# Taking the level products of a gated linear recurrence in two halves of 64 stationary columns

## The chip, the cores and the metric

The kernel runs on one core of one Trainium2 chip. The metric is the device time of one execution in microseconds (us). Engines: TensorE (PE in the profile; its weight loads are a row of their own, PEld), VectorE (DVE), ScalarE (ACT), GpSimd (POOL), and SyncE (SP), which issues most DMAs.

## The reference: what is computed

A decoder trunk of two layers on x of 512 tokens by 1024 channels, float32. Layer 0 mixes tokens by an mLSTM and channels by a dense SwiGLU; layer 1 mixes tokens by an HGRN2 recurrence and channels by eight SwiGLU experts of which each token takes two. The part that matters here is the recurrence of layer 1, eight heads with keys and values of 128. In the reference, cut to what matters:

```python
def hgrn2_chunkwise(q, k, log_f, v):
    def step(s_st, xs):
        qc, kc, gc, vc = xs
        bc = jnp.cumsum(gc, axis=2)
        diff = bc[:, :, :, None, :] - bc[:, :, None, :, :]
        decay = jnp.exp(jnp.where(mask[:, :, None], diff, NEG))
        a = jnp.einsum('bhtd,bhsd,bhtsd->bhts', qc, kc, decay)
        o = (jnp.einsum('bhtd,bhdv->bhtv', qc * jnp.exp(bc), s_st)
             + jnp.einsum('bhts,bhsv->bhtv', a, vc))
        ...
```

The scores a[t, s] need a decay per channel d between tokens s and t, so they aren't one matrix product.

## The kernel before, in words

**Whole program.** Activations lie channel by token, 512 tokens in the free dimension. Each float32 weight block is split into two float32r parts (whi on ScalarE, wlo on VectorE), and a product of weights and activations is three matmuls with 512 columns. `Weights` (line 165) loads the blocks through SyncE's queue in the order of use and emits their splits. [...]

**The HGRN stage** (`hgrn`, line 1014, some 680 to 930 us of the span). `proj` (line 1071) is the main stream of wide matmuls: projections in the order v0, h2, h4, v1, h6, g0, g4 (names hv, hh, hg in the trace), then the output product h_out. After each pair of heads is projected, `evac` (line 1040) makes q, k, and the log of the forget gate summed within chunks of 128 tokens. `core` (line 1124) is one head's recurrence: it is emitted in steps between those of the main stream.

**A head's levels.** Within a chunk, the scores are built by halves: for n = 1, 2, 4, ..., 64, the pairs whose s lies in the left half and t in the right half of a block of 2n tokens. The seven levels are run by `skew` in four stages. `l0` (line 1160): E, two VectorE subtractions of 128x256 and an exp on ScalarE. `l1_` (line 1173): M = E times the left halves' k and the right halves' q, one VectorE instruction of 128x512. `l2_` (line 1179): for each of the four chunks one float32 product into the PSUM tile lp (al in the trace). Its stationary operand is the chunk's 128 columns of M (for n = 1, of k), its moving operand the 64 columns of right halves, and its result 128 x 64. For n = 64 only the 64 left columns are stationary. `l3` (line 1193): a copy of the wanted entries of lp into A by a mask, VectorE, 128x256. A float32 matmul shows as two records in the trace, each with a load of its own.

After the levels come the outputs (o) and the state (su, St) chunk by chunk, a norm by head on ScalarE, a transposition (tph), and hh, the head's operand of h_out. `heads` (line 1250) splits hh into hhi (ScalarE) and hlo (VectorE).

**What sets the order.** `weave` (line 336) emits the main stream and, between its steps of six wide matmuls, steps of up to three heads. It goes by `Plan` (line 270), which adds up the cost of what it gave to each engine:

```python
        if engine == "tensor":
            return n * (1.667 if out.dtype == F32 and ins[0].dtype == F32 else 0.417) * 1e-3
```

where n is the number of columns of the matmul's output. VectorE is charged 0.07 us and 1.04 or 0.53 ns per column, by the operands. A head's step is emitted if its previous step ends by the plan 0.3 us before TensorE's clock, and if the plan's VectorE and ScalarE are less than 3 us behind TensorE's:

```python
            late = max(t["vector"], t["scalar"]) - t["tensor"]
            if not x[2] and x[0] <= t["tensor"] + slack and late < backlog:
```

**Another place with halves.** In the mLSTM's `pair` (line 837), line 897 writes two products of 64 stationary columns to `cu[0:64]` and `cu[64:128]`.

All instructions of TensorE, VectorE and ScalarE go through one helper (line 317), so the trace tells them apart by tile and not by line.

Of the kernel before, what the change touches and what calls it, by code (L numbers as in the profile page):

```python
# [19 lines left out]
DRAM = bass.MemoryType.DRAM  # L20
# [17 lines left out]
# ---------------------------------------------------------------- weight order  # L38
# Every product's weights are cut into [128, 128] blocks and laid out in the order of use.
# [46 lines left out]
# ---------------------------------------------------------------- column vectors  # L86
# [14 lines left out]
def _consts():  # L101
    """Constants that depend on shapes alone, side by side in columns."""
# [39 lines left out]
def moe_steps():  # L142
    """The experts' products in order: an expert's first gate and up tiles go before the last one's down."""
    for e in range(NE + 1):
        if e < NE:
            yield from (("g", e, f) for f in range(EARLY))
        if e:
            yield from (("d", e - 1, d) for d in range(KT))
        if e < NE:
            yield from (("g", e, f) for f in range(EARLY, ET))  # L150


def moe_order():
    """Loads of the experts' weights: slots of gate and up tiles, then of the down product."""
    for e in range(NE + 1):
        if e < NE:
            yield from ((e * MB // 8 + 2 * f, 2) for f in range(EARLY))
        if e:
            base = (e - 1) * MB // 8 + 2 * ET
            yield from ((base + i, min(2, ET - i)) for i in range(0, ET, 2))  # L160
        if e < NE:
            yield from ((e * MB // 8 + 2 * f, 2) for f in range(EARLY, ET))


class Weights:
    """The weight blocks, loaded in pairs of slots and split into two float32r parts each.

    A slot of eight blocks is also a tick: what `at` puts off is emitted with the split of a later slot."""
# [20 lines left out]
    def want(self, slot):  # L189
        """Splits up to this slot, as far as room is free; returns what is left to emit."""  # L190
# [19 lines left out]
    def at(self, n, f):  # L210
        """Emits f n ticks from now."""
        self.tasks.setdefault(self.now + n, []).append(f)
# [11 lines left out]
    def rush(self, n=8):  # L224
        """The next n splits as far as there is room, where much other work is to come. Nothing that uses a
        block is left to emit."""
# [7 lines left out]
    def get(self, b, n=1, last=True):  # L234
        """Blocks b to b + n in two parts. Their slot's room is free again after its last block's last use."""
# [22 lines left out]
def skew(n, *stages, back=False):  # L258
    """Stage s of item k goes with stage 0 of item k + s, after it or (back) before it."""
# [10 lines left out]
class Plan:  # L270
    """Estimates of when each engine would get done with what it was given; `weave` goes by them."""
# [35 lines left out]
class Engine:  # L307
    """An engine whose instructions the plan takes note of."""
# [15 lines left out]
class Core:  # L324
    """nc with its compute engines seen by a plan."""
# [10 lines left out]
def weave(plan, main, sides, lanes, slack, backlog):  # L336
    """Emits main and, between its steps, those of the sides, `lanes` of them at a time.

    A side is a pair: whether it can start, and its steps. A step goes when by the plan the one before is
    done about when the tensor engine gets to it, and the other engines aren't too far behind.  # L340
    A side that yields "wait" needs more of main first, and main that does needs more of the sides."""
# [46 lines left out]
class Kernel:  # L388
# [15 lines left out]
    # ------------------------------------------------------------ small helpers  # L404
# [18 lines left out]
    def rsqrt(self, v, pool, name):  # L423
        """v ** -0.5 of a small tile: the exponent's halving for a start, then Newton's steps."""
# [9 lines left out]
    def table(self, name):  # L434
        """Loads a table set of the scalar engine's functions; Exp and Ln go by the one they find."""
# [6 lines left out]
    def dump(self, name, tiles):  # L442
        """For tests: [P, n] tiles side by side into a DRAM output."""
# [19 lines left out]
    def mm2(self, acc, w, x, start, stop):  # L463
        """acc[:, 0] + acc[:, 1] is the product; x has its two parts side by side."""
# [4 lines left out]
    # ------------------------------------------------------------ start  # L469
# [23 lines left out]
    # ------------------------------------------------------------ conditioning  # L493
    def scale_of(self, l, i, s=slice(0, 8)):
        """A = (1 + scale) * norm_w, for a layer's i-th norm."""
# [3 lines left out]
    def times_c(self, out, t):  # L499
        """A column of the sums of t * silu(c) by row."""  # L500
# [5 lines left out]
    def ada_first(self, pool):  # L506
        """Stages for shift and scale of the first norm, a d-tile at a time."""
# [5 lines left out]
        # (1 + scale) * norm_w with the bias' share first  # L513
# [55 lines left out]
    # ------------------------------------------------------------ norm  # L569
    def square(self, k):  # L570
        """The squares that the next norm takes: those before the last d-tile's as a sum, and the last's."""
# [12 lines left out]
    def token_scale(self):  # L584
        """1 / sqrt(mean square + eps), a column by token tile."""
# [11 lines left out]
    def norm(self, l, i, before=()):  # L597
        """hn = x * rs * A + B by d-tile, split into two float32r parts."""
# [36 lines left out]
    # ------------------------------------------------------------ products  # L635
    def group_first(self, name, n, normed):
        """n accumulators in step with a norm's d-tiles."""
# [10 lines left out]
    def tile_ws(self, b, xs, acc):  # L648
        """One 128-column tile of a product, d-major: weights stationary."""
# [6 lines left out]
    def tile_tok(self, b, i, acc):  # L656
        """Token tile i by 512 columns: tokens stationary."""
# [11 lines left out]
    def out_proj(self, name, hh, l, side=lambda: None):  # L669
        """x += gate1 * (hh @ w_out); hh gives the operands in turn, or None where they aren't there yet.  # L670
        Steps of side go along at last."""
# [36 lines left out]
    def to_dmajor(self, tp, w, pool, name):  # L708
        """A head's d-major outputs, times w, split."""
# [7 lines left out]
    # ------------------------------------------------------------ layer 0: mLSTM  # L717
    def mlstm(self):
# [3 lines left out]
        with ExitStack() as ctx:  # L722
# [24 lines left out]
            # q, k: convolution over four taps, silu  # L747
# [12 lines left out]
            # gates: rows 0-7 input gates, 32-39 forget gates  # L760
# [76 lines left out]
            def pair(p):  # L837
                """Two heads; then their outputs, gated and d-major."""
# [94 lines left out]
            def close(h):  # L933
                """A head's outputs, normed and gated, d-major."""
# [32 lines left out]
    # ------------------------------------------------------------ layer 0: dense SwiGLU  # L967
# [45 lines left out]
    # ------------------------------------------------------------ layer 1: HGRN2  # L1013
    def hgrn(self):
# [3 lines left out]
        with ExitStack() as ctx:  # L1018
# [8 lines left out]
            # lower bound: softmax over the one layer, its running sum less the first  # L1027
# [12 lines left out]
            def evac(n, qf):  # L1040
                """Two heads' q, k, log f summed within chunks, and q * f of the odd tokens."""
# [11 lines left out]
                for s in range(2):  # L1053
# [5 lines left out]
                    # log f; the table's range is narrower than the floor's  # L1059
# [50 lines left out]
            def gated(hs):  # L1110
                """The gates of some heads, and the outputs that were there before them."""
# [7 lines left out]
            def sel(qk, h):  # L1119
                """By level h: k of the left halves and q of the right ones."""  # L1120
# [3 lines left out]
            def core(h):  # L1124
# [7 lines left out]
                # across chunks  # L1132
# [8 lines left out]
                # within chunks: the diagonal, then halves of 1, 2, 4, ... tokens  # L1141
# [37 lines left out]
                def l2_(i):  # L1179
# [8 lines left out]
                    m = 64 if n == 64 else P  # L1188
                    for c in range(NC):
                        nc.tensor.matmul(lp[:m, c * 64:(c + 1) * 64], left[:, c * P:c * P + m],  # L1190
                                         right[:, c * bn:(c + 1) * bn], start=True, stop=True)
# [15 lines left out]
                # outputs and state  # L1207
# [68 lines left out]
    # ------------------------------------------------------------ layer 1: experts  # L1276
    def router(self):
        """hn @ router = rs * (x @ (A * router)) + B @ router"""
# [7 lines left out]
    def pre_route(self, pool, lps, xt):  # L1286
        """The router's share of x @ router by token, and x by token, as x's d-tiles get done."""
# [6 lines left out]
        def logits(k):  # L1294
            """By expert: x's d-tiles before the last; by token: their sum turned, and the last."""
# [53 lines left out]
    def route(self, pool, lps, xt):  # L1349
        """Top two experts of a token, its gates, and its rows in the experts' lists."""  # L1350
# [31 lines left out]
        # the first expert's rows straight from x by token: a product picks them and scales them  # L1382
# [6 lines left out]
        def picks(e, i, w):  # L1389
            """Row by row, which of a tile's tokens is in it, times w."""  # L1390
# [7 lines left out]
        def spread():  # L1398
            """Tokens to their rows of the experts' lists."""
# [36 lines left out]
        def rest(sl, ok, gate):  # L1436
            # what goes past an expert's rows
# [16 lines left out]
            # gates and rows of the last expert's results, and of the others'  # L1454
# [56 lines left out]
    def overflow(self, xt):  # L1511
        """Tokens past their expert's rows: each expert on all tokens, with the gates of those alone."""
# [47 lines left out]
    def experts(self, xp, hp, wk, xt, pick, rest):  # L1560
# [6 lines left out]
        def fetch(e):  # L1567
            """An expert's rows."""
# [10 lines left out]
        def turn(e, k0, kn):  # L1579
            """Its rows d-major, scaled and shifted, in two parts."""  # L1580
# [32 lines left out]
        def act(e, f, gu):  # L1613
            """silu(gate) * up, in two parts."""
# [24 lines left out]
        def down(e, d, yp):  # L1639
            """gate2 times a d-tile of the result, its rows by token at last."""  # L1640
# [46 lines left out]
        def select():  # L1687
            """The last expert's rows as the columns of products that add them to their tokens."""
# [13 lines left out]
        def add(i, j):  # L1702
            """What the experts before the last give a token."""
# [45 lines left out]
    def finish(self, rp, xt, g, r):  # L1749
        """The last expert's share, and the final norm."""  # L1750
# [55 lines left out]
# ---------------------------------------------------------------- host: layout only  # L1806
# [54 lines left out]
```

## Time and profile before

| | |
|---|---|
| time, median of 3 runs | 1597.63 us (1595.0, 1597.63, 1610.0) |
| span of the profiled execution | 1596.0 us |
| time of the profiled execution around its span | not given by the page |
| mean granted clock of TensorE | 0.975 |
| TensorE busy | 1526.0 us, 96% |
| VectorE busy | 1087.0 us, 68% |
| ScalarE busy | 843.7 us, 53% |

A row of the timeline has the start in us from the span's start, the time from the start of its first instruction to the end of its last, the engine, the line, the operation, the tiles written and read, the rows and columns of the array in use, the moving operand or the load, and how many neighbouring instructions the row merges (x8). Ends of matmuls are modelled; starts are measured, so intervals are best taken from start to start.

### The profile page before, as it was taken

Reading aid. Unit: us, or ns where it says so; the run is one execution under the profiler, and the core shown is the slowest. Engines: PE = TensorE matmul, PEld = TensorE weight load, DVE = VectorE, ACT = ScalarE, POOL = GpSimd, SP = SyncE. Lnnn points to the kernel's source line nnn. Section 1 sums busy time; section 2 is a strip of 40 time slices with the busy share of each in tenths; the row PEclk is TensorE's granted clock in tenths of the full one; section 3 lists DMA queues with packets and bytes.
Section 4 is the critical chain, followed back from the end, with each engine's and each line's share of the span. In section 5 each row is a group of like instructions: output and inputs, shape, how many; then the busy total and the mean of one; then the engine's idle time right before and its main releaser. Section 6 shows DMA issues by size and latency. Waiting matters only on the chain. (4 is left out here: it accounts for less than half of the span.)

```text
span 1596.0 us, 23645 instructions
## 1 busy us (share of the span) xinstructions
PE 1526.0 (96%) x8991; PEld 1326.5 (83%) x8991; DVE 1087.0 (68%) x1981; ACT 843.7 (53%) x1560; POOL 118.5 (7%) x187
## 2 busy tenths in 40 slices
PE   4989989999999999999999998999999999999995
PEld 3866767788888888688888876999999999999994
DVE  6875684555445555595977644787877777787794
ACT  5463533432213322365656534777776767777663
POOL 0000000000000000300000010401001010100152
PEclk9999999999999999999999998999999999999996
DMA  9322452254455553532102132877777786877772
GB/s 378 149 96 90 145 191 100 105 219 178 171 195 182 191 194 111 206 141 89 54 28 79 54 133 88 332 258 276 266 261 275 251 294 227 292 257 251 275 284 89
DMA packets 79542, 297.30 MB, mean 186 GB/s; under 512 B 7732, under 2 KB 7780, under 8 KB 78400
## 3 DMA queue, kind: packets, MB, share of 16 engines
q1 hardware_dynamic: 69424, 266.36, 46.6%
q0 software_dynamic: 10000, 29.38, 5.3%
q8 instruction: 73, 1.20, 0.3%
q14 instruction: 45, 0.37, 0.1%
HBM read 277.64 MB, written 18.06 MB: 185 GB/s over the span
## 5 line engine op out<-in xcount | busy, mean ns | idle before, releaser
L317 DVE TENSOR_TENSOR wlo<-raw,whi 128x1024 fp32r<-128x1024 f32 x403 | 490.2, 1223 | 129.4 <-ACT whi L317 128.0
L317 ACT ACTIVATE whi<-raw 128x1024 fp32r<-128x1024 f32 x403 | 422.1, 1055 | 183.8 <-DMA raw<-in_w 39.4
L317 PE MATMUL gu<-x,whi 128*128 128x304 f32 x1408 | 359.0, 344 | 1.0 <-DVE x L317 1.0
L317 PE MATMUL gu<-x,wlo 128*128 128x152 f32 x1408 | 327.8, 233 | 0.0
L317 PEld LDWEIGHTS gu<-x,wlo 128*128 128x128 f32 x1408 | 269.0, 191 | 0.0
L317 PEld LDWEIGHTS gu<-x,whi 128*128 128x128 f32 x1408 | 264.3, 188 | 1.9 <-DVE x L317 1.1
L317 PE MATMUL yd<-h,whi 128*128 128x304 f32 x704 | 184.3, 350 | 2.8 <-DVE h L317 2.8
L317 PE MATMUL yd<-h,wlo 128*128 128x152 f32 x704 | 164.9, 234 | 0.0
L317 PEld LDWEIGHTS yd<-h,whi 128*128 128x128 f32 x704 | 133.9, 190 | 3.3 <-DVE h L317 3.2
L317 PEld LDWEIGHTS yd<-h,wlo 128*128 128x128 f32 x704 | 136.2, 194 | 0.0
L317 DVE SCALAR_TENSOR_TENSOR ar<-ar,cond 128x1024 f32<-128x1024 f32 x80 | 97.2, 1218 | 6.9 <-DMA ar<-in_ada 6.9
L317 ACT ACTIVATE fhi<-fg 128x512 fp32r<-128x512 f32 x22 | 13.9, 633 | 114.3 <-DVE fg L317 114.3
L317 DVE TENSOR_TENSOR fg<-fg,fup 128x512 f32<-128x512 f32 x20 | 13.8, 688 | 82.6 <-PE fup L317 82.6
L317 PE MATMUL fd<-fhi,whi 128*128 128x512 f32 x176 | 69.6, 396 | 0.0
L317 PE MATMUL fd<-flo,whi 128*128 128x512 f32 x176 | 69.6, 396 | 0.0
L317 PE MATMUL fd<-fhi,wlo 128*128 128x512 f32 x176 | 69.6, 396 | 0.0
L317 ACT ACTIVATE t<-gu 128x152 f32<-128x152 f32 x176 | 48.5, 288 | 34.5 <-PE gu L317 34.5
L317 PE MATMUL fgp<-lo,whi 128*128 128x512 f32 x160 | 62.3, 389 | 0.0
L317 PE MATMUL fgp<-hi,whi 128*128 128x512 f32 x160 | 62.2, 389 | 0.0
L317 PE MATMUL fgp<-hi,wlo 128*128 128x512 f32 x160 | 62.2, 389 | 0.0
L317 PE MATMUL fup<-hi,whi 128*128 128x512 f32 x160 | 62.2, 389 | 0.0
L317 PE MATMUL fup<-lo,whi 128*128 128x512 f32 x160 | 62.2, 389 | 0.0
(408 smaller groups left out, 3015.3 us busy)
## 6 DMA issues: line engine op xcount, KB each, us to landing
raw<-in_moe SPq DMA_DIRECT2D x128, 1024.0 KB, 5.3
raw<-in_w SPq DMA_DIRECT2D x69, 1024.0 KB, 4.9
ar<-in_ada SPq DMA_DIRECT2D x80, 512.0 KB, 4.2
ad<-in_ada SPq DMA_DIRECT2D x8, 1024.0 KB, 17.4
XG<-zero POOLq DMA_DIRECT2D x18, 256.0 KB, 5.9
raw<-in_moe SPq DMA_DIRECT2D x8, 512.0 KB, 3.5
xr<-XG POOLq DMA_DIRECT2D x14, 256.0 KB, 6.2
Y<-yt POOLq DMA_DIRECT2D x14, 256.0 KB, 3.8
```

What stands on the lines that cost most here:

```text
L317: r = f(*args, **kw)
```

## The change

The product of each chunk is issued for 64 columns of the stationary operand at a time: the first half writes partitions 0 to 63 of lp, the second 64 to 127. The moving operand is the same for both. For n = 64 the product stays one of 64 columns. The copies that read lp stay as they were. The rest of the diff takes out comments and docstrings.

```diff
                     lp = Ls[i] = self.ps(f"al{n}{h}", (P, 256))
                     bn = P // (2 * n)
-                    m = 64 if n == 64 else P
                     for c in range(NC):
-                        nc.tensor.matmul(lp[:m, c * 64:(c + 1) * 64], left[:, c * P:c * P + m],
-                                         right[:, c * bn:(c + 1) * bn], start=True, stop=True)
+                        for m in range(0, 64 if n == 64 else P, 64):
+                            nc.tensor.matmul(lp[m:m + 64, c * 64:(c + 1) * 64], left[:, c * P + m:c * P + m + 64],
+                                             right[:, c * bn:(c + 1) * bn], start=True, stop=True)
```

## Rows read from the trace of the kernel before

**Rows 1.** The page, busy time, share and instructions of the engines.
```profile
PE 1526.0 (96%) x8991; PEld 1326.5 (83%) x8991; DVE 1087.0 (68%) x1981; ACT 843.7 (53%) x1560; POOL 118.5 (7%) x187
```

**Rows 2.** Stretches: PE, PEld, DVE, ACT, POOL busy, granted clock, DMA share, GB/s.
```profile
700.00:720.00 20.00, 20.00 (x125) 17.37 (x124) 18.89 (x40) 10.16 (x15) 0.00 (x0) 1.00 0.15 54
720.00:740.00 20.00, 20.00 (x120) 17.30 (x119) 7.10 (x26) 5.72 (x26) 0.00 (x0) 1.00 0.15 54
...
920.00:940.00 20.00, 17.73 (x71) 13.90 (x71) 11.28 (x21) 9.36 (x23) 4.17 (x9) 0.91 0.51 177
```

**Rows 3.** Tile al: records, ns min/median/max, first and last start, forms.
```profile
L317 PE MATMUL al<-M x384: 217/275/325, 697.6 to 906.4; 128*128 128x64 f32 x160, 128*64 128x64 f32 x32
L317 PEld LDWEIGHTS al<-q,QK x64: 188/192/192, 695.2 to 876.5; 128*128 128x128 f32 x64
```

**Rows 4.** Timeline, ends of a stretch of 128 columns; ends and loads of one of 64.
```profile
715.07 0.39 PE L317 MATMUL hh<-hi,wlo 128*128 128x512 f32 x1
...
716.43 0.39 PE L317 MATMUL hh<-lo,whi 128*128 128x512 f32 x1
...
717.36 0.40 PE L317 MATMUL hh<-hi,wlo 128*128 128x512 f32 x1
717.68 0.54 PEld L317 LDWEIGHTS al<-M 128*64 128x64 f32 x8 [0.36 <-issue]
...
718.63 0.40 PE L317 MATMUL hh<-lo,whi 128*128 128x512 f32 x1
```

**Rows 5.** Timeline, a stretch of two 128-column groups.
```profile
707.34 0.40 PE L317 MATMUL hv<-whi,lo 128*128 128x512 f32 x1
...
707.58 1.89 PE L317 MATMUL al<-M 128*128 128x64 f32 x16
...
709.59 0.39 PE L317 MATMUL hv<-wlo,hi 128*128 128x512 f32 x1
```

**Rows 6.** Timeline of TensorE, the wide matmuls around the mixed stretch.
```profile
825.59 0.40 PE L317 MATMUL hh<-hi,wlo 128*128 128x512 f32 x1
...
827.75 0.40 PE L317 MATMUL hh<-lo,whi 128*128 128x512 f32 x1
```

**Rows 7.** Tile cu, loads (ns); then its first four records in three windows.
```profile
L317 PEld LDWEIGHTS cu<-va,kt x48: 132/134/137, 117.6 to 173.1; 128*64 128x64 f32 x48
...
117.63 0.20 PEld L317 LDWEIGHTS cu<-va,kt 128*64 128x64 f32 x4 [0.36 <-issue]
...
117.64 0.33 PE L317 MATMUL cu<-va,kt 128*64 128x129 f32 x2
...
117.69 0.14 PEld L317 LDWEIGHTS cu<-va,kt 128*64 128x64 f32 x2
```

**Rows 8.** Timeline of VectorE, the parts of a level's step and two M tiles.
```profile
714.77 0.43 DVE L317 COPY_PREDICATED A<-lvm,al 128x256 f32<-128x256 uint32 x1
...
715.10 0.68 DVE L317 TENSOR_TENSOR M<-E,QK 128x512 f32<-128x512 f32 x1
...
715.70 0.75 DVE L317 TENSOR_TENSOR E<-LF 128x256 f32<-128x256 f32 x2
...
761.36 0.69 DVE L317 TENSOR_TENSOR M<-E,QK 128x512 f32<-128x512 f32 x1 [0.70 <-ACT E L317]
```

**Rows 9.** Timeline of TensorE, two groups of level products.
```profile
721.17 1.00 PE L317 MATMUL al<-M 128*128 128x64 f32 x8
...
763.17 1.00 PE L317 MATMUL al<-M 128*128 128x64 f32 x8
```

**Rows 10.** Waits from 690 to 910 us: us in total, times, longest.
```profile
PEld al L317 <- DVE M L317: 0.4, 1, 0.4
```

**Rows 11.** Timeline of TensorE, the end of the stage.
```profile
924.91 0.49 PE L317 MATMUL h_out<-hhi,whi 128*128 128x512 f32 x1 [1.80 <-ACT hhi L317]
...
926.21 0.62 PE L317 MATMUL h_out<-hhi,whi 128*128 128x512 f32 x1
926.63 0.63 PE L317 MATMUL h_out<-hlo,whi 128*128 128x512 f32 x1
```

## The prediction

> **What bounds the kernel now.** I read the page's busy times first. TensorE is busy for 96% of the span and no other engine passes 68% [rows 1]. That is an average, so the next view is the table of 20 us stretches over the HGRN stage, where the touched products run. [...] The stage is bound by TensorE's instruction stream, and time taken out of that stream shortens the kernel unless TensorE then waits for something else.
>
> Next come the level products themselves. The answer for the tile al counts 384 records for the levels of 2 to 64 tokens and 64 for the level of 1; the forms stand 5 to 1, so 320 + 64 of them load 128 stationary columns and 64 already load 64 [rows 3]. A level has four products (one per chunk of 128 tokens), so the 448 records of 56 levels are eight each: a float32 product is two passes, each with its own load. The change touches every level but the last of a head, 6 levels x 8 heads = 48 groups of eight records. In the order of TensorE's matmuls the 56 groups stand in 48 unbroken stretches, from 695.2 to 906.4 us [rows 3]: 33 stretches of one touched group, 7 of two touched groups back to back, 1 of a 64-column group and a touched one, 7 of a 64-column group alone (33 + 14 + 1 = 48).
>
> **What one stretch costs today.** I measure from the start of the last 512-column matmul ahead of a stretch to the start of the second one behind it; so the load that the stretch exposes is counted. One touched group: 715.07 to 716.43, 1.36 us. A 64-column group in the same surroundings: 717.36 to 718.63, 1.27 us [rows 4]. Two touched groups: 707.34 to 709.59, 2.25 us [rows 5]. The mixed stretch: 825.59 to 827.75, 2.16 us [rows 6]. Undisturbed, a step of wide matmuls is 0.233 us (716.43 to 717.36 are four [rows 4]), two are 0.47.
>
> Where the time goes differs. In the wide form a step takes about 0.11 us (the double stretch adds 2.25 - 1.36 = 0.89 for eight). In the 64-column form eight loads take 0.54 us [rows 4] and one of that form 0.134 [rows 7], so a step is (0.54 - 0.134) / 7 = 0.058 us. That is 8 x (0.11 - 0.058) = 0.42 us less; but what is left of the stretch, entry and exit, is 1.27 - 8 x 0.058 = 0.81 us against 1.36 - 0.89 = 0.47 [rows 4, 5]. So narrow loads halve the step and pay about 0.34 us per stretch for the change of form and back: the first load starts 0.32 us behind the last wide matmul, so nothing is loaded ahead.
>
> **The change, part by part.**
>
> *Twice the products.* Each touched group issues 16 records in place of 8. If the two halves run one behind the other, a group takes 16 x 0.058 = 0.93 us plus the change of form. If they run together, it takes eight steps, as the 64-column group does. The trace has the same layout at another place: the mLSTM's state update cu writes two 64-column products to the lower and the upper 64 partitions. Its four loads (two halves, two passes) lie within 0.20 us; one behind the other they would take 3 x 0.058 + 0.134 = 0.31. A narrower look shows the last two loads, from 117.69 on, lasting 0.14 together, as long as one of them; so two start at once [rows 7]. So the halves load and stream side by side, and I price a touched group as the 64-column group: 1.27 us, eight steps of 0.058. Bounds: together 1.27, one behind the other 1.27 + 8 x 0.058 = 1.73. I take the lower, since the cu rows are the same form on the same engine; what they don't show is a row of sixteen.
>
> *The sum for the stream.* One touched group: 1.36 - 1.27 = 0.09 saved. Two touched groups: 1.27 + 8 x 0.058 = 1.73 in place of 2.25, 0.52 saved, since the change of form is paid once for both. Mixed: 1.73 in place of 2.16, 0.43 saved. 33 x 0.09 + 7 x 0.52 + 0.43 = 3.0 + 3.6 + 0.4 = 7.0 us, if the stretches stay as they are.
>
> *The planner's clock.* The order is not fixed: weave emits a head's step when the plan says that its last results are done and VectorE is not over 3 us behind. The plan charges a float32 product 1.667 ns per column of its output (line 285), so a touched group is charged 4 x 64 x 1.667 = 0.43 us now and 0.85 after. Its clock of TensorE will run 0.43 us further with each of the 48 groups, 20 us in all, and steps will be emitted earlier in the stream of wide products. Two things follow. First, more groups may fall back to back, which is worth up to 0.34 us for each two single ones that join (2 x 1.27 - 1.73 = 0.81 less the 0.47 of wide matmuls counted twice). Second, VectorE gets less time ahead of each group. A step costs it E 0.75, M 0.68 and A 0.43 us [rows 8], 1.86 together, against 2.29 us from group to group on TensorE (715.07 to 717.36, a group and six wide matmuls [rows 4]); and where the groups are dense it is already busy 18.9 us of 20 [rows 2]. What hides this today is a lead: M of 761.36 ends at 762.05 and its group starts at 763.17, 1.1 us later [rows 8, 9]; the M of 715.10 ends at 715.78 and is used by the group at 721.17, 5.4 us later (the M tiles and their groups run in the same order) [rows 8, 9]. All waits of TensorE for M come to 0.4 us [rows 10]. The lead grows because the plan charges 1.28 + 0.43 = 1.71 us for what takes 2.29; after the change it charges 2.13 for about 2.2, and the lead should stay near its first value instead of growing. Bounds: nothing at all, or a wait at each of the 48 groups of the shortfall worked out under the rivals. I take 1 us of waits and 1 us gained by more joined groups, which cancel.
>
> *What else.* No DMA, no tile and no instruction of VectorE or ScalarE is added; the copies that read the products keep their count and shape. 48 x 8 more matmul records stand against 8991 [rows 1], 4%, each with a load, and their time is in the terms above.
>
> **Sum.** Against the profiled execution, 1596.0 - 7.0 = 1589.0 us. The page gives its span and no other time; the median of the runs, 1597.6, stands 1.6 above it and the fastest run 1.0 below it, so I put the forecast at 1590.0. Its own range is 1585 to 1595.
>
> **Rivals.** *The halves take turns.* Then every touched group costs 8 x 0.058 = 0.46 us more than I priced: 48 x 0.46 = 22, less the 7.0, is 15 slower, about 1612. For it: no row has 16 such records in a row. Against it: the cu rows. The same time would come out if a load had to wait for the product before it in its own half, for a step then is load and product in turn, 0.116 us. [...] Our trace disagrees: the second loads of cu start at 117.69, 0.05 us into a pair of matmuls of 0.33 [rows 7], and eight 64-column loads follow each other in 0.54 us [rows 4].
>
> *TensorE waits for M (the slower side).* If the earlier emission packs two groups between six wide matmuls, TensorE needs (1.40 + 1.26) / 2 = 1.33 us per group (six steps of 0.233, and 1.73 less 0.47), VectorE 1.86: 0.53 us short at each. Twelve levels of a pair of heads make 6.4 us, less a lead of 1 to 5, say 3, so 3.4 us for each of four pairs, 14 us, against which the saving of 7 stands: about 1603. It decides from 7 us of waits on. For it: VectorE's 18.9 us of 20 [rows 2]. Against: the plan counts VectorE too, and by prices close to the measured ones (E 0.67, M 0.60 and A 0.34 by the prices of lines 292 and 293, 1.61 us for 1.86), so it won't emit much faster than VectorE can follow.
>
> [...]
>
> **How the numbers follow.** Forecast 0.56; the better tail 0.20; waits for M 0.18; turns 0.06. The range from 1582 to 1602 takes in the tail and most of the waits and leaves out the turns and the ends of the other two, some 0.15 to 0.2. About 1%, 16 us, is what a measurement of this kernel tells from no change. Faster than 1581.6 needs the tail and twice the joined groups: 0.05. Slower than 1613.6 needs turns and waits together: 0.04. Within: 0.91. Faster by a little is far likelier than slower by a little.
>
> **What would show it.** The al rows should count 832 matmul records (48 x 16 + 8 x 8), all of 128 x 64 form, their loads at 0.13 to 0.14 us with 16 of them lying within some 0.6 us; 1.2 us would mean turns. A stretch between wide matmuls should measure 1.27 or, for a double one, 1.73. Stretches should be fewer than 48. Waits of TensorE for M should stay under 3 us; 7 or more make the forecast wrong, as would a stretch of one group above 1.4 us. [...]

## The result, and the profile after

The changed kernel takes 1622.45 us (median of four runs, 1620.27 to 1624.84) against 1597.7 (median of four, 1595.0 to 1610.0). The recorded ratio is 1.0121, 95% interval 1.0075 to 1.0167 (the two medians alone give 1.0155): slower, and outside the range. The forecast was 1590, range 1582 to 1602. Two of the twelve later runs of the changed kernel were in a slower state, and they are left out of its time and ratio below.

The page of the changed kernel, and the answer for tile al, answer to [rows 1] and [rows 3]:

```profile
PE 1538.3 (95%) x9375; PEld 1321.0 (81%) x9375; DVE 1086.4 (67%) x1981; ACT 841.4 (52%) x1558; POOL 119.5 (7%) x187
```

```profile
L317 PE MATMUL al<-M x704: 218/222/274, 709.6 to 921.3; 128*64 128x64 f32 x176
L317 PE MATMUL al<-q,QK x128: 218/222/271, 707.4 to 899.0; 128*64 128x64 f32 x128
```

The 384 added records are there: 704 + 128 = 832, all in the 128*64 form. One stretch of a touched group, from the timeline, beside [rows 4]:

```profile
714.09 0.39 PE L317 MATMUL hv<-whi,lo 128*128 128x512 f32 x1
714.40 0.55 PEld L317 LDWEIGHTS al<-M 128*64 128x64 f32 x16 [0.36 <-issue]
...
715.36 0.40 PE L317 MATMUL hv<-wlo,hi 128*128 128x512 f32 x1
```

Sixteen loads lie within 0.55 us, where eight took 0.54, and the stretch measures 715.36 - 714.09 = 1.27 us, the value that was worked out. The array does what the change says. (With the order of before, in the first experiment below, 20 undisturbed stretches of one group measure 1.26 to 1.29 us and seven of two groups 1.73 to 1.75.) So where did 27.1 us of span (1623.1 - 1596.0) come from? The timeline of TensorE gives the times at which the stage starts (the router's first matmul, bps) and ends (the first transposition behind the output product, xt). In the kernel before:

```profile
678.75 0.95 PE L317 MATMUL bps<-rw,mod 128*128 128x8 f32 x8
...
958.23 0.60 PE L317 MATMUL xt<-cst_c,xr 128*128 128x128 f32 x4
```

and in the changed one:

```profile
690.77 0.95 PE L317 MATMUL bps<-rw,mod 128*128 128x8 f32 x8
...
986.17 0.60 PE L317 MATMUL xt<-cst_c,xr 128*128 128x128 f32 x4
```

Ahead of the stage 12.0 us are lost, in the stage 295.4 - 279.5 = 15.9, and behind it 0.8 are won. The first 12.0 lie in the mLSTM, where TensorE's instructions are the same in both kernels: its step from the projection v to o stands at 165.25 us before and at 177.38 after. The table of 20 us stretches, first before and then after, shows a spell at a lower granted clock, 0.50 (in windows of 1 us it is 0.50 from 140 to 166 us of the changed kernel):

```profile
140.00:160.00 20.00, 20.00 (x86) 14.39 (x85) 9.16 (x19) 1.20 (x2) 0.00 (x0) 0.91 0.24 81
160.00:180.00 20.00, 20.00 (x115) 15.46 (x114) 12.71 (x42) 14.50 (x46) 0.63 (x2) 1.00 0.28 91
```

```profile
140.00:160.00 20.00, 20.00 (x57) 13.51 (x55) 5.33 (x10) 1.21 (x4) 0.00 (x0) 0.50 0.09 26
160.00:180.00 20.00, 20.00 (x78) 15.23 (x78) 8.71 (x14) 5.98 (x8) 0.00 (x0) 0.83 0.31 103
```

That spell turns out below to come and go from execution to execution, so the experiments are judged by the stage, from bps to xt.

In the stage, these are TensorE's waits in the changed kernel, us in total, times, longest. PE is the row of matmuls and PEld that of loads; the kernel before had 0.4 for M on the row of loads [rows 10] and none on the other:

```profile
PEld al L317 <- DVE M L317: 9.0, 20, 1.1
...
PE ad L317 <- DVE QK L317: 6.7, 4, 2.2
...
PE al L317 <- DVE M L317: 5.6, 15, 0.9
...
PE hkp L317 <- DVE kl L317: 2.7, 1, 2.7
...
PE tph L317 <- ACT qi L317: 1.9, 2, 1.4
PE h_out L317 <- ACT hhi L317: 1.9, 1, 1.9
```

Two places stand out. Level products wait for M, as in this piece of the timeline, where M of 720.13 ends at 720.81 and its group starts 0.06 later, against leads of 1.1 to 5.4 us before [rows 8, 9]:

```profile
719.65 0.69 PE L317 MATMUL al<-M 128*64 128x64 f32 x16
...
720.13 0.68 DVE L317 TENSOR_TENSOR M<-E,QK 128x512 f32<-128x512 f32 x1
...
720.87 0.69 PE L317 MATMUL al<-M 128*64 128x64 f32 x16 [0.54 <-DVE M L317]
```

And at the start of the second and the fourth pair of heads TensorE stands idle until evac has made QK (at the third, until kl is made, a step later: the one wait of hkp above), and its granted clock falls from 1.00 to 0.50. The timeline of the second pair and the table of stretches:

```profile
761.08 0.39 PE L317 MATMUL hh<-hi,wlo 128*128 128x512 f32 x1
763.61 1.60 PE L317 MATMUL ad<-QK 128*128 128x128 f32 x8 [2.15 <-DVE QK L317]
766.19 2.08 PE L317 MATMUL ad<-QK 128*128 128x128 f32 x8 [0.98 <-DVE QK L317]
```

```profile
752.00:772.00 20.00, 16.87 (x70) 13.79 (x69) 12.76 (x21) 14.36 (x25) 0.00 (x0) 0.83 0.25 97
...
812.00:832.00 20.00, 16.62 (x99) 13.26 (x100) 12.17 (x34) 13.09 (x43) 0.00 (x0) 0.91 0.00 0
...
872.00:892.00 20.00, 16.40 (x67) 13.38 (x66) 14.55 (x25) 14.45 (x26) 0.00 (x0) 0.83 0.29 106
...
952.00:972.00 20.00, 20.00 (x83) 16.37 (x82) 8.19 (x11) 6.11 (x9) 5.44 (x13) 0.92 0.63 218
```

The first three are the pair starts. In windows of 1 us the granted clock of these stretches is 1.00 or 0.50, and between the two only where it changes: at the second pair it is 1.00 until 764 us, 0.58 in the next window, 0.50 from 765 to 771, and 1.00 again. At 0.50 the wide matmuls start 0.43 us apart (768.50 to 770.63), where they are 0.23 apart at 1.00 (758.13 to 761.08). The means of 0.83, 0.91 and 0.83 are 6.8, 3.6 and 6.8 us at 0.50, since 1 - 0.83 = 0.17 is half of the share of time at it. The last is the end of the stage, another 3.2 us, as in the kernel before ([rows 2], 0.91): 20.4 us in all, where the kernel before has 3.6.

### The profile page after: what moved, and what is told of

It reads as the page before. It is cut to its first block, busy times and chain, and to the rows that moved or that the text cites. A ratio compares the mean times of both kernels' runs of the same rounds, so it can differ in the third digit from the quotient of the medians.

```text
span 1623.1 us, 24422 instructions
## 1 busy us (share of the span) xinstructions
PE 1538.3 (95%) x9375; PEld 1321.0 (81%) x9375; DVE 1086.4 (67%) x1981; ACT 841.4 (52%) x1558; POOL 119.5 (7%) x187
## 5 line engine op out<-in xcount | busy, mean ns | idle before, releaser
L317 DVE TENSOR_TENSOR wlo<-raw,whi 128x1024 fp32r<-128x1024 f32 x403 | 489.9, 1222 | 148.1 <-ACT whi L317 146.9
L317 ACT ACTIVATE whi<-raw 128x1024 fp32r<-128x1024 f32 x403 | 422.1, 1055 | 196.5 <-DMA raw<-in_w 41.4
L317 PE MATMUL gu<-x,whi 128*128 128x304 f32 x1408 | 359.0, 344 | 1.0 <-DVE x L317 1.0
L317 PE MATMUL gu<-x,wlo 128*128 128x152 f32 x1408 | 327.8, 233 | 0.0
L317 PEld LDWEIGHTS gu<-x,wlo 128*128 128x128 f32 x1408 | 269.0, 191 | 0.0
L317 PEld LDWEIGHTS gu<-x,whi 128*128 128x128 f32 x1408 | 264.3, 188 | 1.9 <-DVE x L317 1.1
L317 PE MATMUL yd<-h,whi 128*128 128x304 f32 x704 | 181.6, 346 | 2.5 <-DVE h L317 2.5
L317 PE MATMUL yd<-h,wlo 128*128 128x152 f32 x704 | 163.9, 233 | 0.0
L317 PEld LDWEIGHTS yd<-h,whi 128*128 128x128 f32 x704 | 132.2, 188 | 2.9 <-DVE h L317 2.9
L317 PEld LDWEIGHTS yd<-h,wlo 128*128 128x128 f32 x704 | 134.6, 191 | 0.0
L317 DVE SCALAR_TENSOR_TENSOR ar<-ar,cond 128x1024 f32<-128x1024 f32 x80 | 97.2, 1218 | 5.4 <-DMA ar<-in_ada 5.4
L317 ACT ACTIVATE fhi<-fg 128x512 fp32r<-128x512 f32 x22 | 13.9, 633 | 114.3 <-DVE fg L317 114.3
L317 PE MATMUL fd<-fhi,whi 128*128 128x512 f32 x176 | 69.6, 396 | 0.0
L317 PE MATMUL fd<-flo,whi 128*128 128x512 f32 x176 | 69.6, 396 | 0.0
L317 PE MATMUL fd<-fhi,wlo 128*128 128x512 f32 x176 | 69.6, 396 | 0.0
L317 DVE TENSOR_TENSOR fg<-fg,fup 128x512 f32<-128x512 f32 x20 | 13.8, 688 | 82.7 <-PE fup L317 82.7
L317 ACT ACTIVATE t<-gu 128x152 f32<-128x152 f32 x176 | 48.6, 289 | 34.4 <-PE gu L317 34.4
L317 PE MATMUL fgp<-lo,whi 128*128 128x512 f32 x160 | 62.3, 389 | 0.0
L317 PE MATMUL fgp<-hi,whi 128*128 128x512 f32 x160 | 62.2, 389 | 0.0
L317 PE MATMUL fgp<-hi,wlo 128*128 128x512 f32 x160 | 62.2, 389 | 0.0
L317 PE MATMUL fup<-hi,whi 128*128 128x512 f32 x160 | 62.2, 389 | 0.0
L317 PE MATMUL fup<-lo,whi 128*128 128x512 f32 x160 | 62.2, 389 | 0.0
```

Of the source, the lines that this page charges most:

```text
L317: r = f(*args, **kw)
```

## The experiments

The time of the kernel before differs from chip to chip (medians of 1597.7, 1603.5, 1617.6 and 1617.3 us), so each ratio is to its runs on the same chip.

**The array and the order, taken apart.** One kernel keeps the halves and hides the second half from the planner; the other keeps the wide products and charges the planner twice. The first of them ("the old price" below):

```diff
-                            nc.tensor.matmul(lp[m:m + 64, ...
+                            mm = nc.tensor._engine.matmul if m else nc.tensor.matmul
+                            mm(lp[m:m + 64, ...
```

> The changed products, but the planner is charged for the first half alone, 0.43 us a group as before the change, so that everything is emitted in the order of before. Stage: from the first bps matmul to the first gu matmul, 321.2 us before and 338.4 after. Theory A (the doubled price reorders the stage, and the waits of the new order cost what the array gives and more): the stage takes 314 us (321.2 less 7.0), waits of TensorE for M stay under 2 us, and the time is 1590 us. Theory B (the narrow form itself is the loss, by its switches or by what it does to the clock): the stage takes 330 us or more and the time is 1605 or more. Theory C on the 12 us that the changed kernel lost before the stage, at the same instructions (a long spell at the lower clock from about 140 us on): it comes by chance from run to run, so it is here in some executions and not in others; if it belongs to the changed program, it is here in all.

Measured: 1598.22 us against 1603.46 of the kernel before, ratio 0.9981 (0.9953 to 1.0008), which by itself doesn't tell the two apart.

```profile
691.23 0.73 PE L317 MATMUL bps<-rw,mod 128*128 128x8 f32 x6
...
964.28 0.60 PE L317 MATMUL xt<-cst_c,xr 128*128 128x128 f32 x4
```

The stage takes 273.1 us, 6.4 less than before (by the measure of the expectation, to gu, 314.6 where 314 was expected): the stream's saving of 7.0 was nearly right, and theory B is out. Its waits in the stage, on the row of matmuls (for M the row of loads has 3.9):

```profile
PE ad L317 <- DVE QK L317: 1.8, 2, 1.1
...
PE h_out L317 <- ACT hhi L317: 1.6, 2, 1.4
...
PE al L317 <- DVE M L317: 1.1, 2, 0.8
...
PE hkp L317 <- DVE kl L317: 0.7, 1, 0.7
```

The other kernel:

```diff
+                        if m == P:
+                            nc.plan.note("tensor", "matmul", (lp[:m, ...], left[...], right[...]), {})
```

> The products of before with 128 stationary columns, but the planner is charged twice for each touched group, 0.85 us, so that everything is emitted in the order of the changed kernel. Theory A: the waits come with the order, so the stage takes 335 to 345 us in place of 321.2, and the time is 1611 to 1620. Theory B: the order costs nothing, the stage takes 320 to 324 us and the time is 1596 to 1600. Theory C: as in the other run, the spell at the lower clock around 140 us is there in some executions and not in others.

Measured: 1621.5 us, ratio 1.0132 (1.0085 to 1.0178).

```profile
686.11 0.73 PE L317 MATMUL bps<-rw,mod 128*128 128x8 f32 x6
...
981.93 0.60 PE L317 MATMUL xt<-cst_c,xr 128*128 128x128 f32 x4
```

The stage takes 295.8 us, 16.3 more than before, with not one product changed. So the loss is the order, theory A. Of the 16.3 us, 7.2 are more idle time of TensorE (13.4 against 6.2) and 9.1 are slower work with the same instructions; the stretches at the pair starts have granted clocks of 0.83, 0.91 and 0.83, as in the changed kernel. As to theory C, the early spell is there in the profiles of both kernels (granted clock 0.50 and 0.54 from 140 to 160 us) and not in that of the next one (0.91). In this kernel the waits for M come to 0.5 us only, though:

```profile
PE ad L317 <- DVE QK L317: 5.4, 4, 2.2
...
PE hkp L317 <- DVE kl L317: 2.7, 1, 2.7
...
PE al L317 <- DVE M L317: 0.5, 1, 0.5
```

Its longest waits stand at the pair starts. In the new order the narrow products bring nothing (295.4 against 295.8): TensorE is busy 7.8 us less (274.6 against 282.4) and idle 7.3 us more, of which 5.1 are waits for M.

**How far ahead the other half may stand.** As the run with the old price, with the two loops exchanged (all first halves of a group, then all second ones):

```diff
-                    for c in range(NC):
-                        for m in range(0, 64 if n == 64 else P, 64):
+                    for m in range(0, 64 if n == 64 else P, 64):
+                        for c in range(NC):
```

> As the run with the old price, but a group issues the first half of all four chunks (eight records) and then the second half of all four (eight records), in place of the halves of a chunk in turn. If TensorE starts a record of the other half only when it stands within a few records of the one in progress, the eight records of each half follow each other, a group of sixteen takes 0.93 us from first to last start in place of 0.46, and the time is 22 us above the run with the old price, about 1612 us. If it looks eight and more records ahead, there is no difference.

Measured: ratio 1.0034 (1.0001 to 1.0066), the stage 962.64 - 678.85 = 283.8 us, 10.7 more than with the halves in turn. Neither end of the expectation. The second halves have a line of their own (L1192) in these two kernels; a group here, and the same with the halves in turn:

```profile
701.02 0.50 PE L317 MATMUL al<-M 128*64 128x64 f32 x5
701.31 0.27 PE L1192 MATMUL al<-M 128*64 128x64 f32 x1
701.36 0.22 PE L317 MATMUL al<-M 128*64 128x64 f32 x1
701.42 0.22 PE L1192 MATMUL al<-M 128*64 128x64 f32 x1
```

```profile
712.72 0.27 PE L317 MATMUL al<-M 128*64 128x64 f32 x1
712.73 0.27 PE L1192 MATMUL al<-M 128*64 128x64 f32 x1
712.83 0.22 PE L317 MATMUL al<-M 128*64 128x64 f32 x1
712.83 0.22 PE L1192 MATMUL al<-M 128*64 128x64 f32 x1
```

In turn, each record starts within 0.01 us of its twin. Apart, the first five records of the first half start one by one (the last at 701.02 + 0.50 - 0.22 = 701.30), and the ninth in program order starts at 701.31, with the fifth and ahead of the sixth at 701.36. In 26 of the 33 stretches of one group the records stand exactly so. From the last wide matmul ahead to the second one behind, the group takes 702.26 - 700.70 = 1.56 us here and 713.67 - 712.39 = 1.28 with the halves in turn.

**More cover at a pair's start.** The changed kernel, in which a pair may start only four steps of the main stream after its evac:

```diff
-            weave(nc.plan, main(), [(lambda h=h: h in LF, core(h)) ...
+            weave(nc.plan, main(), [(lambda h=h: h in LF and tick[0] >= born[h], core(h)) ...
```

(tick counts the steps of the main stream, and born is set to four steps behind a pair's evac.)

> The changed kernel with its doubled price, but from the second pair on a pair of heads may start only four steps of the main stream (24 wide matmuls) after its evac; in the changed kernel 12 wide matmuls lay between, in the one before 24. Theory A (at each start of a pair TensorE runs dry, since too few wide matmuls cover the evac, and its clock falls): waits of ad for QK, 12.1 us in the changed kernel over both rows, come to 5 or less, the lower clock takes less than 8 us in the stage in place of 20.5, the stage takes 324 to 330 us in place of 338.4, and the time is about 1610. Theory B (the waits for M alone are the loss): the stage stays above 334 us, the time at 1618 or more.

Measured: ratio 1.0059 (1.0032 to 1.0087); the stage takes 977.09 - 685.39 = 291.7 us, 3.7 less than in the changed kernel, 334.7 by the measure to gu. A miss, though two of the signs of theory A came: the waits for QK are gone, and the time at a granted clock of 0.50 falls to 6.8 us by the table of stretches. But other waits took their place:

```profile
PE al L317 <- DVE M L317: 7.7, 14, 1.4
PE hkp L317 <- DVE kl L317: 7.2, 3, 2.8
...
PE o L317 <- DVE A L317: 2.7, 1, 2.7
```

TensorE is idle for 22.5 us of this stage, 1.7 more than in the changed kernel (20.8). A later start moved the idle time to the next steps of the same chain, and what the stage gained was the clock.

**All prices as measured.** The changed kernel, with the planner's prices in the stage set to what the trace shows:

```diff
+            if self.measured:
+                if n == 64:
+                    return 0.1
+                return n * (1.667 if out.dtype == F32 and ins[0].dtype == F32 else 0.455) * 1e-3
...
-            return 0.15 + n * 0.83e-3 + 1.28 * load
+            return (0.2 if self.measured else 0.15) + n * 0.83e-3 + 1.28 * load
...
-        return 0.07 + n * (
+        return (0.16 if self.measured else 0.07) + n * (
```

> The changed kernel, but within the stage the planner charges what the trace shows: 0.1 us for a product of 64 columns (0.8 a group), 0.455 ns a column of a wide matmul in place of 0.417, and 0.09 us more for each VectorE and 0.05 us more for each ScalarE instruction. Theory A (the doubled price hurts since it speeds up the plan's TensorE against a VectorE that is priced some 14% too low; the old price was too low on both sides): the stage takes 312 to 320 us, near the 314.6 of the run with the old price. Rival (a plan that steps the heads earlier is worse at any consistent prices, since packed steps leave the pair ends bare): the stage takes 326 us or more.

Measured: ratio 0.9999 (0.9962 to 1.0035); the stage takes 956.96 - 678.47 = 278.5 us, and 321.5 to gu, between the two bounds of the expectation and nearer to theory A: 16.9 of the 22.3 us between the changed kernel (295.4) and the old price (273.1) come back with a group still charged 0.8 us. So the doubled price hurt chiefly because it stood beside prices that are too low; the run set those of VectorE, ScalarE and the wide matmuls right together and doesn't tell them apart. Why the rest remains is open; TensorE's waits for hhi and hlo at the stage's end are 5.0 us here against 2.1 with the old price, so part of it is a later end of the heads against the output product.

**Cheaper still.** Halves, charged for two chunks only, 0.21 us a group:

```diff
-                            mm = nc.tensor._engine.matmul if m else nc.tensor.matmul
+                            mm = nc.tensor._engine.matmul if m or c > 1 else nc.tensor.matmul
```

> The changed products, charged 0.21 us a group, half of the price of before and a quarter of that of the changed kernel. If stepping the heads later is only good, the stage takes less than the 314.6 us of the run with the old price, by 2 us or more. If the price of before lies near an optimum, heads now end too late for the output product, waits for hhi at the end of the stage grow from 3.9 us, and the stage takes 318 us or more.

Measured: ratio 1.0001 (0.9966 to 1.0036); the stage takes 958.55 - 679.14 = 279.4 us, 6.4 more than at the old price (321.2 to gu). The old price is the best of the three (quarter, old, doubled), and what was expected of a lower one came: the heads end too late, and h_out waits:

```profile
PE h_out L317 <- ACT hhi L317: 4.5, 3, 1.9
...
PE h_out L317 <- DVE hlo L317: 3.5, 6, 1.2
```

**Fewer changes of form.** The old price, with a head's products issued two levels at a time:

```diff
-                for _ in skew(len(levels), l0, l1_, l2_, l3, back=True):
+                for _ in skew(len(levels), l0, l1_, l2_, lambda i: None, l3, back=True):
```

(and l2_ does nothing for even levels and both for odd ones).

> The run with the old price, but a head's products are issued two levels at a time (six of the seven levels in three pairs), with their copies one step later. If the change of form and back is a cost per stretch, 24 stretches fall away at 0.34 us each, 8 us: stage 306 to 309 us, time 8 below the run with the old price. Rival: the later copies delay each head, or M tiles run short, and waits of TensorE take it back: stage 314 us or more.

Measured: ratio 1.0006 (0.9974 to 1.0037); the stage takes 972.80 - 690.17 = 282.6 us, 9.6 more than without. Stretches fell to 30 and TensorE's busy time by 1.8 us (265.4 against 267.2), but it waited 4.1 us at once for QK ahead of a projection, and 2.8 for M. The rival was right in the outcome; the longest wait, for QK, it hadn't named.

**Idle time filled.** The changed kernel, with wide matmuls that nobody reads in place of the idle time at a pair's start:

```diff
                 ad = self.ps(f"ad{h}")
+                for k in range((5 if h % 2 else 11) if h > 1 else 0):
+                    nc.tensor._engine.matmul(ad, self.hn[k % KT][0][:, 0:P], self.hn[k % KT][0], start=True, stop=True)
```

> The changed kernel, with wide matmuls that nobody reads written into the tile ad ahead of its products from the second pair of heads on, 11 at a pair's first head and 5 at its second, about 2.6 and 1.2 us, where TensorE idles today for 2.5 and 1.4. Their result is overwritten and the planner is not charged. Theory A (part of the loss is the lower clock that follows these idle spells: 17 us more of it in the stage than before, 8.5 us of time): the lower clock disappears from the three pair starts, and the time from the first bps to the first xt matmul falls from 295.4 us to 286 to 290. Rival (the idle spells cost only themselves): 295 us or more.

Measured: ratio 1.0037 (1.0011 to 1.0063); the stage takes 979.93 - 690.67 = 289.3 us, 6.1 less than in the changed kernel, by adding work. The same stretches as above:

```profile
752.00:772.00 20.00, 19.79 (x96) 16.34 (x95) 12.83 (x21) 14.44 (x25) 0.00 (x0) 1.00 0.27 99
812.00:832.00 20.00, 19.48 (x155) 16.20 (x155) 13.74 (x40) 12.83 (x42) 0.00 (x0) 1.00 0.01 1
872.00:892.00 20.00, 19.80 (x111) 16.25 (x110) 15.38 (x29) 15.08 (x27) 0.00 (x0) 1.00 0.23 80
```

The granted clock is 1.00 in all three pair starts, where it was 0.83, 0.91 and 0.83: theory A. The 6.1 us are what is left of a larger gain. TensorE's busy time in the stage is 276.0 us against 274.6, though 48 matmuls of some 0.23 us, 11 us in all, were added; so the rest took about 10 us less, near the 8.6 us that the pair starts' 17.2 us at 0.50 cost (an estimate: half of them, as the wide matmuls start 0.43 us apart there in place of 0.23). The waits for QK and kl are filled, and those for M grow from 5.6 to 7.6 us.

**The old price and the changed kernel again**, side by side with more rounds.

> The run with the old price once more, with more rounds, beside the changed kernel on the same chip. If the order is the loss, it is 0.3 to 0.6% faster than the kernel before and the stage again takes 6 to 7 us less. If the first result was chance, it is within 0.2%.

Measured: 1606.98 us against 1617.25, ratio 0.9938 (0.9910 to 0.9966); the stage takes 963.54 - 690.48 = 273.1 us, as the first time. Here the gain is clear of noise: the halves with the old price beat both kernels.

> The changed kernel once more, beside the others on the same chip. If the early spell at the lower clock comes by chance, its share is that of the kernel before on this chip, and the ratio to before stays at what the stage loses, 1.010 to 1.012; if the spell belongs to the changed kernel, the ratio is above 1.015.

Measured: 1624.7 us (median of ten runs), ratio 1.0053 (1.0019 to 1.0086), less than either expectation. Its profiled execution doesn't have the early spell, with the same program as the first time:

```profile
140.00:160.00 20.00, 20.00 (x93) 14.68 (x93) 9.75 (x19) 2.17 (x5) 0.00 (x0) 1.00 0.26 82
160.00:180.00 20.00, 20.00 (x116) 15.46 (x115) 13.21 (x45) 13.92 (x46) 0.63 (x2) 1.00 0.28 100
```

The stage takes 974.11 - 678.84 = 295.3 us, as in the first profile. So the early spell isn't the change's; the 15.9 us of the stage are, 1.0% of the time. The measured ratios, 1.0121 and 1.0053, lie on either side of that, and their intervals overlap. That they differ by the share of executions with the spell is likely but not shown: each group of runs has one trace.

## Why the prediction was wrong, point by point

- *One stretch and the sum for the stream:* right. 1.27 us per touched group and 1.73 to 1.75 for two, as worked out, and 6.4 us gained in the stage where the sum was 7.0, once the order is held. The mechanism, two halves that load and stream side by side, held for sixteen records as it did for cu's four (sixteen loads in 0.55 us, each record within 0.01 us of its twin); the rival of halves in turn is out.
- *The planner's clock:* this is the step that failed. It said that the lead would stay near its first value and took 1 us of waits against 1 us of joined groups. The direction of the price was seen and its effect on the place of groups too (the 48 stretches became 33), but the price of the new order was 22.3 us (295.4 with it, 273.1 without). TensorE is busy for 274.6 us of the one and 267.2 us of the other, so 14.9 us are more idle time and 7.4 us slower work with the same instructions, less what the fewer changes of form give back. The idle time is, by the waits above, M 4.5, ad for QK 4.9, hkp 2.0, tph 1.9 and o 1.4 us more. For the slower work the lower clock is enough: 20.4 us at a granted clock of 0.50 in the changed kernel's stage against 3.6 in the kernel before, whose order the old price keeps, of which half the difference, 8.4 us, is lost (an estimate, as if TensorE worked at half its pace all that time). The premise behind the step was that the plan's prices of VectorE are close to the measured ones (1.61 for 1.86 us), so that it wouldn't emit much faster than VectorE can follow; with all prices as measured, 16.9 of the 22.3 us came back.
- *The rival of waits for M* had the sign and the right place for a part. By the row of loads, on which the prediction counted, M's waits grew from 0.4 to 9.0 us, past the 7 that it named. They are real, but the run with the price alone has next to none of them and loses 16.3 us all the same. What no case held was the start of a pair: the second pair is let in 12 wide matmuls behind its evac where there were 24, as is the fourth, and evac isn't done. Why is read from the code and wasn't tried by itself: heads that step earlier finish earlier and leave the plan's VectorE with little pending, so its lag stays under the limit of weave. The place was in sight, for ad waited 1.8 us already before the change; besides M the prediction looked only at the waits at the end of the stage.
- *The better tail, priced at 0.20:* no run shows it as a gain. In the kernel before, h_out's first matmul behind the last wait stands idle 1.80 us for hhi, and from 926.21 on eight intervals between wide matmuls are 0.42 us in place of 0.23 [rows 11]. After the change h_out's waits for hhi fell from 3.2 to 1.9 us, but the slow matmuls stayed (granted clock 0.92 from 952 to 972 us, 0.43 us from start to start), and this was small beside the pair starts.
- *The sum's base:* the forecast started from the profiled execution without the early spell. The four runs of the changed kernel have granted clocks of 0.964 to 0.966 and its profiled one has the spell; the 12 us of it are in the profiles' difference and not in the change. Without them the stage alone, 15.9 us, would have put the time at about 1613 (an estimate), still outside the range.
- *The order of records.* In the run with the halves apart TensorE's records don't all start in the order of emission (ends are modelled in these traces): all calls of L317 come first in a group, yet a record of L1192 starts at 701.31, ahead of one of L317 at 701.36.

## What to carry to other kernels

Where a planner's prices set the order of emission, a change of the instruction count is a change of the order: hold the order first (here, by hiding the added instructions from the plan), measure the edit, and then reprice all engines together. A price that is wrong may be balanced by others that are wrong the same way; setting one of them alone cost 22.3 us here, where the edit gave 6.4. Column halves with float32 operands ran side by side when they were issued in turn (sixteen loads in 0.55 us, where eight had taken 0.54); a step fell from 0.11 to 0.058 us, and the change of form took most of it back unless several groups stood in a row (0.09 us gained on one group, 0.5 on two).

## What the runs showed of the hardware that was not expected

- Records of two 64-column halves started within 0.01 us of each other when they were neighbours in the order; with eight records of the first half ahead of it, the second half started only with the fifth of them, and a group cost 0.28 us more.
- Waits of TensorE of 2.2 and 1.0 us at one pair's start, 2.2 and 1.4 at another and 2.7 at a third came with 6.8, 6.8 and 3.6 us at a granted clock of 0.50; with useless matmuls in them the granted clock of these stretches was 1.00 and the stage became 6.1 us shorter.
- From 140 to 160 us the granted clock is 0.50 in one execution of the changed kernel and 1.00 in another. Between the profiles of the two kernels, with 0.50 and 0.91 there, some 12 us were lost.
